# Key sums of stick-breaking attention in four products per head, a low-rank gate weight in one stationary block, and two gate rows spread by way of DRAM

## The chip, the cores and the metric

The kernel runs on one core of one Trainium2 chip. The metric is the device time of one execution in microseconds (us), as the median of several runs. Five engines work side by side, each in its own program order: TensorE (PE, the matrix products; its weight loads are listed as PEld), VectorE (DVE), ScalarE (ACT), GpSimd (POOL) and SyncE (SP, which here only starts transfers, one after the other).

## The reference, cut to what matters

One layer: adaLN modulation from a vector `c`, two token mixers side by side (gated linear attention, "GLA", and stick-breaking attention), an output projection, then a squared-ReLU MLP. 256 tokens, width 2048, all in float32.

```python
mod = silu(c) @ w_ada + b_ada;  sh1, sc1, g1, sh2, sc2, g2 = split(mod, 6)
h = rmsnorm(x, ng[0]) * (1 + sc1) + sh1
proj = h @ w_in               # q_a k_a v_a r_a a_low q_b k_b v_b gate_a gate_b
# GLA: log_a = log_sigmoid(a_low @ w_gate_up + b_gate) / 16   (a_low has 16 columns)
# stick-breaking, 16 heads of 128, query blocks of 128:
z = q @ k.T * 128 ** -0.5
log_1mb = where(past, log_sigmoid(-z), 0)
after = cumsum(log_1mb, reverse over keys) - log_1mb
w = where(past, exp(log_sigmoid(z) + after), 0);  o = w @ v
mixed = sigmoid(gate_a) * y_a + sigmoid(gate_b) * y_b
x = x + g1 * rmsnorm(mixed @ w_out, ng[1])
f = square(relu((rmsnorm(x, ng[2]) * (1 + sc2) + sh2) @ w_ff1)) @ w_ff2
x = x + g2 * rmsnorm(f, ng[3])
```

## The kernel before

Every float32 operand of a large product is split into a high part `h_...` (ACT, line 156) and a low part `l_...` (DVE, line 157). `mm_b_split` (line 166) does 16 steps over the inner dimension with two products each: the high weight block against 512 columns (256 tokens high, then 256 low) and the low weight block against the 256 high columns. `natural_block` (line 208) does three products of 512 columns per step. The weights come in loads of 1 MB started by SP (`load`, line 140) into the pool `wraw` with four buffers; their split halves go to the pool `wsp` with five buffers of each kind. A load waits on SP until the DVE has finished with the buffer that it takes. The modulation vector is worked out by DVE in 96 steps (`ada_step`, line 300, tiles `ad`) that are strewn between the products. A scheduler arranges each engine's order when the program is built; on the chip each engine keeps to it.

In order of time: the products of v and r (tile `pv`); the low-rank gate (lines 447 to 496); q and k of GLA per head (`pb_qa`, `pb_ka`); the GLA gates and outputs; q and k of stick-breaking (`pb_qb`, `pb_kb`) with the stages `sb_scores`, `sb_weights`, `sb_values` of earlier heads between them; the second gate and output (`pa_gb`, `pa_yb`); `w_out` (`pa_wo`); the MLP in eight parts (`pb_f`, `pa_f`).

Three places are touched.

**Key sums** (`sb_weights`, line 639). For each head, suffix sums over keys are products with a triangular matrix `uinc_r` and a matrix of ones, each for the high and the low part of `nl`. PSUM tile `pc` holds 384 columns: keys 0 to 127 against all 256 queries in columns 0 to 255, keys 128 to 255 against queries 128 to 255 in columns 256 to 383.

**Low-rank gate** (lines 448 to 480). The weight `a_low` of 16 columns is laid into zeroed blocks of 128 columns, high part `wl_h` and low part `wl_l`, and multiplied with `mm_b_split` (tile `pb_al`). The sum `alT` (16 rows and a row of ones for the bias) is the stationary operand of four products with `gup_sb` (tiles `gt`); ACT and DVE make `ls` from them, and `eg` are products with `ls`.

**Rows of g1 and g2** (`spread2`, line 280). A vector stands down the partitions (`G1c`, `G2c`, 128 x 16) and is wanted as a row of 2048 on every partition (`G1`, `G2`). DVE makes diagonal matrices `dg` (in a buffer of `wraw`), PE multiplies ones by them (`sp`), ACT copies out. Rows of g1 are first used by `mixed_out` (line 765), rows of g2 by `ff_out` in the last of the eight parts (line 820).

Of the kernel before, what the change touches and what calls it, by code (L numbers as in the profile page):

```python
# [8 lines left out]
F32 = mybir.dt.float32  # L9
F32R = mybir.dt.float32r  # L10
AF = mybir.ActivationFunctionType
ALU = mybir.AluOpType
PSUM = bass.MemoryType.PSUM

P = 128
D = 2048
T = 256
KT = D // P
# [19 lines left out]
def trunk_kernel(ctx, tc, xT, xn, cT, ada, bcol, ngcol, w_alow, w_gup, gg_row,  # L38
# [3 lines left out]
    v_, s_, g_, pe, dma = nc.vector, nc.scalar, nc.gpsimd, nc.tensor, nc.sync  # L42

    const = ctx.enter_context(tc.tile_pool(name="const", bufs=1))
    wraw = ctx.enter_context(tc.tile_pool(name="wraw", bufs=4))
    wsp = ctx.enter_context(tc.tile_pool(name="wsp", bufs=5))
# [10 lines left out]
    def pm(name):  # L57
        return ps_m.tile([P, 512], F32, tag="pm", name=name)

    def pw(name):  # L60
        return ps_w.tile([P, 512], F32, tag="pw", name=name)
# [215 lines left out]
                s_.copy(dst(n), ps[:, m])  # L277
        return made

    def spread2(cols, dst, name):  # L280

        dgs = wraw.tile([P, KT, P], F32R, tag="raw", name=f"dg_{name}")
        hi = const.tile([P, KT], F32R, name=f"ch_{name}")
        lo = const.tile([P, KT], F32, name=f"cl_{name}")
        v_.tensor_copy(hi, cols)
        v_.tensor_tensor(out=lo, in0=cols, in1=hi.bitcast(F32), op=ALU.subtract)
        for n in range(4):
            ps = pm(f"sp_{name}_{n}")
            for u, c in enumerate((hi.bitcast(F32), lo)):
                dg = dgs[:, 8 * (n % 2) + 4 * u:8 * (n % 2) + 4 * u + 4]  # L290
                v_.tensor_tensor(out=dg, in0=ident.unsqueeze(1).broadcast_to([P, 4, P]),
                                 in1=c[:, 4 * n:4 * n + 4].unsqueeze(2).broadcast_to([P, 4, P]), op=ALU.mult)
                pe.matmul(ps, ones_r, dg.rearrange("p k t -> p (k t)"), start=u == 0, stop=u == 1)
            s_.copy(dst(n), ps)

    cb = const.tile([P, D], F32, name="cb")
    with tc.high_priority():
# [147 lines left out]
    gp = ctx.enter_context(ExitStack())  # L445
    gl = gp.enter_context(tc.tile_pool(name="gl", bufs=1))
    if True:
        gup_sb = wraw.tile([P, 2048], F32, tag="raw", name="gup_sb")[0:17, 0:1024]
        s_.dma_start(gup_sb, w_gup)
        wl_r = gl.tile([P, KT, 16], F32, name="wl_r")  # L450
        s_.dma_start(wl_r, w_alow)
        parts = []
        for u in range(2):
            wl_h = wsp.tile([P, 8, P], F32R, tag="hi", name=f"wl_h{u}")
            wl_l = wsp.tile([P, 8, P], F32R, tag="lo", name=f"wl_l{u}")
            g_.memset(wl_h.bitcast(F32), 0.0)
            g_.memset(wl_l.bitcast(F32), 0.0)
            r = wl_r[:, 8 * u:8 * u + 8]
            s_.copy(wl_h[:, :, 0:16], r)
            v_.tensor_tensor(out=wl_l[:, :, 0:16], in0=r, in1=wl_h[:, :, 0:16].bitcast(F32), op=ALU.subtract)  # L460
            parts.append([t.rearrange("p k c -> p (k c)") for t in (wl_h, wl_l)])
        pl = mm_b_split(parts, hT, "al")

        al2 = evp.tile([P, T], F32, tag="e0", name="al2")[0:16]
        s_.copy(al2, pl[0:16, T:2 * T])
        alT = evp.tile([P, T], F32, tag="e1", name="alT", bufs=1)[0:17]
        v_.memset(alT, 1.0)
        v_.tensor_tensor(out=alT[0:16], in0=pl[0:16, 0:T], in1=al2, op=ALU.add)

        ls = [slot([1024], f"ls{i}") for i in range(NTOK)]  # L470
        for i in range(NTOK):
# [140 lines left out]
    with tc.tile_pool(name="sb", bufs=3) as sb:  # L612
        def sb_project(h):
            qk = []
            for w, nm in ((w_qb, "q"), (w_kb, "k")):
                t = sb.tile([P, T], F32, tag=f"s{nm}", name=f"s{nm}_{h}", bufs=2)
                ps = mm_b(w[h], hT, f"{nm}b_{h}")
                merge(t, ps, f"{nm}b_{h}", float(P) ** -0.5 if nm == "q" else None)
                ada_tick()
                qk.append(t)  # L620
            return qk

        def sb_scores(h, q, k):
            pz = pm(f"pz_{h}")
            pe.matmul(pz[:, 0:T], k[:, 0:P], q, start=True, stop=True)
            pe.matmul(pz[:, T:384], k[:, P:T], q[:, P:T], start=True, stop=True)
            z = sb.tile([P, 384], F32, tag="z", name=f"z_{h}", bufs=2)
            v_.tensor_tensor(out=z, in0=pz[:, 0:384], in1=negm, op=ALU.add)
            e = sb.tile([P, 384], F32, tag="e", name=f"e_{h}")
            s_.activation(e, z, AF.Abs)  # L630
            s_.activation(e, e, AF.Exp, scale=-1.0)
            s_.activation(e, e, AF.Ln, bias=onec)
            v_.scalar_tensor_tensor(out=e, in0=z, scalar=0.0, in1=e, op0=ALU.max, op1=ALU.add)
            nl = sb.tile([P, 2, 384], F32R, tag="nl", name=f"nl_{h}", bufs=2)
            s_.copy(nl[:, 0], e)
            v_.tensor_tensor(out=nl[:, 1], in0=e, in1=nl[:, 0].bitcast(F32), op=ALU.subtract)
            return z, e, nl

        def sb_weights(h, z, e, nl):
            pc = pm(f"pc_{h}")  # L640
            for u in range(2):
                pe.matmul(pc[:, 0:T], uinc_r, nl[:, u, 0:T], start=u == 0, stop=False)
            for u in range(2):
                pe.matmul(pc[:, P:T], ones_r, nl[:, u, T:384], start=False, stop=u == 1)
            for u in range(2):
                pe.matmul(pc[:, T:384], uinc_r, nl[:, u, T:384], start=u == 0, stop=u == 1)
            v_.scalar_tensor_tensor(out=z, in0=pc[:, 0:384], scalar=-1.0, in1=z, op0=ALU.mult, op1=ALU.add)
            s_.activation(e, z, AF.Exp)
            return e

        def sb_values(h, e):
            vv, j = vB[h // 4], h % 4
            po = pm(f"pob_{h}")
            pe.matmul(po[:, 0:T], vv[:, 0, j * P:(j + 1) * P], e[:, 0:T], start=True, stop=False)
            pe.matmul(po[:, P:T], vv[:, 1, j * P:(j + 1) * P], e[:, T:384], start=False, stop=True)
            split(oB, h, po[:, 0:T])

        stages = (sb_scores, sb_weights, sb_values)
        held = {}
        for t in range(SBH + 3):  # L660
            if t < SBH:
                held[t] = sb_project(t)
            for n, stage in enumerate(stages, 1):
                h = t - n
                if 0 <= h < SBH:
                    r = stage(h, *held[h])
                    held[h] = r if isinstance(r, tuple) else (r,)
# [42 lines left out]
    def G1(n):  # L710
        return G1t[n // 2][:, n % 2 * 512:(n % 2 + 1) * 512]

    spread2(G1c, G1, "G1")
    ss1 = endp.tile([P, NTOK, 4], F32, name="ss1")
    def rstd(ss, name):

# [65 lines left out]
    for b in range(FB):  # L782
# [23 lines left out]
        if b == FB - 1:  # L806
            while 5 not in done:
                next(jobs)
            G2t = [slot([1024], f"G2{u}") for u in range(2)]
            spread2(G2c, lambda n: G2t[n // 2][:, n % 2 * 512:(n % 2 + 1) * 512], "G2")  # L810
        for n in range(4):
            def ff_out(i, ps):
                f = fs(i, n)
# [83 lines left out]
```

## Time and profile before

| | us |
|---|---|
| median of 3 runs (1822.67 to 1823.84) | 1823.79 |
| the profiled execution, its own time | 1821.68 |
| span of the profiled execution, first to last instruction | 1820.0 |
| TensorE busy | 1780.8 (98%) |
| DVE busy | 1288.3 (71%) |
| ACT busy | 896.8 (49%) |
| POOL busy | 15.8 (1%) |
| moved by DMA | 428.51 MB, mean 235 GB/s |

The busy time of an engine is the time covered by its instructions. Matmuls are pipelined, so the time from the start of one to the start of the next tells what one costs; their own durations overlap. The chain that ended last runs 90% through PE, 5% through DVE and 2% through ACT.

### The profile page before, as it was taken

The numbers are of one execution on the slowest core, as the hardware profiler recorded it, in microseconds if no ns is written. First come the engines' busy times: TensorE is split into PE (matmuls) and PEld (weight loads), VectorE is DVE, ScalarE is ACT, GpSimd is POOL, SyncE is SP. The second block draws the span as 40 slices with busy tenths as digits, with TensorE's granted clock in tenths as the row PEclk, the third lists the DMA queues.
The fourth block names the chain that finished last, engine by engine and source line by source line (L and its number), as shares of the span: only waits on it lengthen the run. The fifth ranks groups of instructions, "written<-read, shape, count | busy, mean of one in ns | idle before, by whom it ended". The sixth has DMA issues, their size and how long they took to land.

```text
span 1820.0 us, 22246 instructions
## 1 busy us (share of the span) xinstructions
PE 1780.8 (98%) x8762; PEld 1485.5 (82%) x8762; DVE 1288.3 (71%) x1516; ACT 896.8 (49%) x1223; POOL 15.8 (1%) x34
## 2 busy tenths in 40 slices
PE   6999999999999999999999999999999999999997
PEld 4787787877888888888888878888888888888886
DVE  8898875887676677776677567676767666656565
ACT  6544544655653465555644455444444343444443
POOL 0000000000000000000000000000000000000000
PEclk8999999999999999999999999999999999999999
DMA  8898964565777766556776643565656666555542
GB/s 334 319 353 324 343 232 184 215 225 221 267 276 272 276 231 232 213 227 254 281 264 229 225 179 139 212 241 218 254 209 236 223 235 231 208 196 187 195 174 81
DMA packets 61179, 428.51 MB, mean 235 GB/s; under 512 B 7169, under 2 KB 7297, under 8 KB 9874
## 3 DMA queue, kind: packets, MB, share of 16 engines
q1 hardware_dynamic: 58896, 422.61, 62.7%
q10 hardware_dynamic: 2178, 4.48, 0.7%
q8 instruction: 69, 1.13, 0.2%
q14 instruction: 36, 0.29, 0.1%
HBM read 424.96 MB, written 2.10 MB: 235 GB/s over the span
## 4 chain that ended last, share of the span: by engine, by line
PE 90%; DVE 5%; issue 2%; ACT 2%; DMA 1%; POOL 0%; SPq 0%; POOLq 0%; DVEq 0%; ACTq 0%
PE pb_f L174 19%; PE pa_f L212 6%; PE pa_f L211 6%; PE pa_f L213 6%; PE pb_kb L174 5%; PE pb_qb L174 5%; PE pv L212 4%; PE pv L213 4%; PE pv L211 3%; PE pb_qa L174 2%; PE pb_ka L174 2%; PE pa_yb L213 2%; PE pa_yb L212 2%; PE pa_yb L211 2%; PE pa_ya L213 2%
## 5 line engine op out<-in xcount | busy, mean ns | idle before, releaser
L157 DVE TENSOR_TENSOR l_f<-r_f,h_f 128x1024 fp32r<-128x1024 f32 x256 | 312.7, 1224 | 181.3 <-ACT h_f L156 178.0
L156 ACT CAST h_f<-r_f 128x1024 fp32r<-128x1024 f32 x256 | 269.2, 1054 | 263.7 <-PE pa_f L213 193.7
L174 PE MATMUL pb_f<-h,h_f 128*128 128x512 f32 x992 | 346.8, 399 | 0.0
L174 PE MATMUL pb_f<-h,l_f 128*128 128x256 f32 x992 | 268.5, 281 | 0.0
L303 DVE SCALAR_TENSOR_TENSOR ad<-ad,cb 128x2048 f32<-128x2048 f32 x96 | 219.1, 2285 | 19.9 <-DMA ad<-in_ada_dram 19.7
L174 PEld LDWEIGHTS pb_f<-h,h_f 128*128 128x128 f32 x992 | 182.7, 188 | 40.4
L211 PE MATMUL pa_f<-h_f,ft 128*128 128x512 f32 x512 | 199.3, 389 | 0.0
L213 PE MATMUL pa_f<-h_f,ft 128*128 128x512 f32 x512 | 199.2, 389 | 0.0
L212 PE MATMUL pa_f<-l_f,ft 128*128 128x512 f32 x512 | 199.2, 389 | 0.0
L174 PEld LDWEIGHTS pb_f<-h,l_f 128*128 128x128 f32 x992 | 187.3, 189 | 6.1
L211 PE MATMUL pv<-h_v,hT 128*128 128x512 f32 x384 | 150.2, 396 | 9.8 <-ACT hT L370 7.1
L212 PE MATMUL pv<-l_v,hT 128*128 128x512 f32 x384 | 151.3, 396 | 3.4 <-DVE l_v L157 3.4
L213 PE MATMUL pv<-h_v,hT 128*128 128x512 f32 x384 | 150.1, 394 | 0.0
L156 ACT CAST h_v<-r_v 128x1024 fp32r<-128x1024 f32 x96 | 98.4, 1047 | 85.1 <-PE pv L213 46.1
L157 DVE TENSOR_TENSOR l_v<-r_v,h_v 128x1024 fp32r<-128x1024 f32 x96 | 115.1, 1219 | 32.6 <-ACT h_v L156 32.4
L213 PEld LDWEIGHTS pa_f<-h_f,ft 128*128 128x128 f32 x512 | 96.1, 188 | 19.9
L212 PEld LDWEIGHTS pa_f<-l_f,ft 128*128 128x128 f32 x512 | 96.1, 188 | 19.9
L211 PEld LDWEIGHTS pa_f<-h_f,ft 128*128 128x128 f32 x512 | 96.1, 188 | 19.8
L211 PEld LDWEIGHTS pv<-h_v,hT 128*128 128x128 f32 x384 | 73.0, 191 | 27.3 <-ACT hT L370 7.5
L174 PE MATMUL pb_qb<-hT,h_qb 128*128 128x512 f32 x256 | 91.7, 399 | 0.0
L174 PE MATMUL pb_kb<-hT,h_kb 128*128 128x512 f32 x256 | 90.6, 393 | 0.0
L212 PEld LDWEIGHTS pv<-l_v,hT 128*128 128x128 f32 x384 | 72.8, 190 | 21.5 <-DVE l_v L157 6.5
(272 smaller groups left out, 3306.2 us busy)
## 6 DMA issues: line engine op xcount, KB each, us to landing
r_f<-in_w_f_dram SPq DMA_DIRECT2D x128, 1024.0 KB, 4.8
ad<-in_ada_dram SPq DMA_DIRECT2D x96, 1024.0 KB, 5.2
r_v<-in_w_nat_dram SPq DMA_DIRECT2D x48, 1024.0 KB, 6.5
r_ga<-in_w_ga_dram SPq DMA_DIRECT2D x16, 1024.0 KB, 5.0
r_ya<-in_w_ao_dram SPq DMA_DIRECT2D x16, 1024.0 KB, 4.8
r_qb<-in_w_qb_dram SPq DMA_DIRECT2D x16, 1024.0 KB, 5.0
r_kb<-in_w_kb_dram SPq DMA_DIRECT2D x16, 1024.0 KB, 5.3
r_gb<-in_w_gb_dram SPq DMA_DIRECT2D x16, 1024.0 KB, 5.1
```

What stands on the lines that cost most here:

```text
L156: s_.copy(hi[:, 0:m], raw[:, o:o + m])
L157: v_.tensor_tensor(out=lo[:, 0:m], in0=raw[:, o:o + m], in1=hi[:, 0:m].bitcast(F32), op=ALU.subtract)
L174: pe.matmul(o, l, r, start=kt == 0 and n == 0, stop=kt == KT - 1 and n == 1)
L211: pe.matmul(ps, ah, w[0], start=start, stop=False)
L212: pe.matmul(ps, ah, w[1], start=False, stop=False)
L213: pe.matmul(ps, al, w[0], start=False, stop=stop)
L303: v_.scalar_tensor_tensor(out=raw, in0=raw, scalar=1.0, in1=cb, op0=ALU.mult, op1=ALU.mult, accum_out=mods[:, m, kt:kt + 1])
```

## The change

`sb_weights` multiplies all 384 columns by the triangular matrix at once, for the high and the low part, and then adds the ones products: four products per head in place of six. The low-rank weight has its high part in columns 0 to 15 and its low part in columns 32 to 47 of one stationary block, so that 16 products of 512 columns do the work of 32; the two results are on partitions 0 to 15 and 32 to 47 and stay apart: `alT` and `gup_sb` now have 48 rows, with the 16 rows of `w_gate_up` twice and zeros between, and the next product adds them. `rows` replaces `spread2`: one transpose to 16 partitions, one copy, one write of 8 KB to DRAM and two transfers that read 4 KB each onto all 128 partitions; all three stand in SP's queue.

```diff
-    def spread2(cols, dst, name):
-
-        dgs = wraw.tile([P, KT, P], F32R, tag="raw", name=f"dg_{name}")
-        hi = const.tile([P, KT], F32R, name=f"ch_{name}")
-        lo = const.tile([P, KT], F32, name=f"cl_{name}")
-        v_.tensor_copy(hi, cols)
-        v_.tensor_tensor(out=lo, in0=cols, in1=hi.bitcast(F32), op=ALU.subtract)
-        for n in range(4):
-            ps = pm(f"sp_{name}_{n}")
-            for u, c in enumerate((hi.bitcast(F32), lo)):
-                dg = dgs[:, 8 * (n % 2) + 4 * u:8 * (n % 2) + 4 * u + 4]
-                v_.tensor_tensor(out=dg, in0=ident.unsqueeze(1).broadcast_to([P, 4, P]),
-                                 in1=c[:, 4 * n:4 * n + 4].unsqueeze(2).broadcast_to([P, 4, P]), op=ALU.mult)
-                pe.matmul(ps, ones_r, dg.rearrange("p k t -> p (k t)"), start=u == 0, stop=u == 1)
-            s_.copy(dst(n), ps)
+    rowp = ctx.enter_context(tc.tile_pool(name="rowp", bufs=1, space=bass.MemoryType.DRAM))
+
+    def rows(cols, dst, name):
+
+        pt = pm(f"rt_{name}")
+        pe.transpose(pt[0:KT, 0:P], cols, ident)
+        t = evp.tile([P, T], F32, tag="half", name=f"rw_{name}")[0:KT, 0:P]
+        s_.copy(t, pt[0:KT, 0:P])
+        d = rowp.tile([KT, P], F32, name=f"rd_{name}")
+        dma.dma_start(d, t)
+        for u in range(2):
+            dma.dma_start(dst[u], d[8 * u:8 * u + 8].rearrange("k p -> (k p)").partition_broadcast(P))
...
-        gup_sb = wraw.tile([P, 2048], F32, tag="raw", name="gup_sb")[0:17, 0:1024]
-        s_.dma_start(gup_sb, w_gup)
+        gup_sb = wraw.tile([P, 2048], F32, tag="raw", name="gup_sb")[0:48, 0:1024]
+        g_.memset(gup_sb, 0.0)
+        s_.dma_start(gup_sb[0:17], w_gup)
+        s_.dma_start(gup_sb[32:48], w_gup[0:16])
         wl_r = gl.tile([P, KT, 16], F32, name="wl_r")
         s_.dma_start(wl_r, w_alow)
-        parts = []
+        pl = pw("pb_al")
         for u in range(2):
-            wl_h = wsp.tile([P, 8, P], F32R, tag="hi", name=f"wl_h{u}")
-            wl_l = wsp.tile([P, 8, P], F32R, tag="lo", name=f"wl_l{u}")
-            g_.memset(wl_h.bitcast(F32), 0.0)
-            g_.memset(wl_l.bitcast(F32), 0.0)
+            wl = wsp.tile([P, 8, P], F32R, tag="hi", name=f"wl{u}")
+            g_.memset(wl.bitcast(F32), 0.0)
             r = wl_r[:, 8 * u:8 * u + 8]
-            s_.copy(wl_h[:, :, 0:16], r)
-            v_.tensor_tensor(out=wl_l[:, :, 0:16], in0=r, in1=wl_h[:, :, 0:16].bitcast(F32), op=ALU.subtract)
-            parts.append([t.rearrange("p k c -> p (k c)") for t in (wl_h, wl_l)])
-        pl = mm_b_split(parts, hT, "al")
+            s_.copy(wl[:, :, 0:16], r)
+            v_.tensor_tensor(out=wl[:, :, 32:48], in0=r, in1=wl[:, :, 0:16].bitcast(F32), op=ALU.subtract)
+            for k in range(8):
+                kt = 8 * u + k
+                pe.matmul(pl, wl[:, k], hT[kt].rearrange("p a t -> p (a t)"), start=kt == 0, stop=kt == KT - 1)
...
-        v_.tensor_tensor(out=alT[0:16], in0=pl[0:16, 0:T], in1=al2, op=ALU.add)
+        for o in (0, 32):
+            v_.tensor_tensor(out=alT[o:o + 16], in0=pl[o:o + 16, 0:T], in1=al2[o:o + 16], op=ALU.add)
...
             for u in range(2):
-                pe.matmul(pc[:, 0:T], uinc_r, nl[:, u, 0:T], start=u == 0, stop=False)
+                pe.matmul(pc[:, 0:384], uinc_r, nl[:, u], start=u == 0, stop=False)
             for u in range(2):
                 pe.matmul(pc[:, P:T], ones_r, nl[:, u, T:384], start=False, stop=u == 1)
-            for u in range(2):
-                pe.matmul(pc[:, T:384], uinc_r, nl[:, u, T:384], start=u == 0, stop=u == 1)
...
-    spread2(G1c, G1, "G1")
+    rows(G1c, G1t, "G1")
...
-            spread2(G2c, lambda n: G2t[n // 2][:, n % 2 * 512:(n % 2 + 1) * 512], "G2")
+            rows(G2c, G2t, "G2")
```

On PE, in the stick-breaking stage, the products of one head's key sums stand between the scores of the next head (`pz`) and the next projection (`pb_qb`). Before:

```order
L626 MATMUL pz_4835<-sq_4628,sk_4675 128x128
L642 MATMUL pc_4848<-nl_4735,uinc_r 128x256 x2
L644 MATMUL pc_4848<-nl_4735,ones_r 128x128 x2
L646 MATMUL pc_4848<-nl_4735,uinc_r 128x128 x2
L174 MATMUL pb_qb_4868<-hT_207,h_qb_0_4860 128x512
```

and of the change:

```order
L626 MATMUL pz_4820<-sq_4613,sk_4660 128x128
L642 MATMUL pc_4833<-nl_4720,uinc_r 128x384 x2
L644 MATMUL pc_4833<-nl_4720,ones_r 128x128 x2
L174 MATMUL pb_qb_4851<-hT_209,h_qb_0_4843 128x512
```

Two products of 128 columns are gone, and the first two have 128 columns more; nothing else moved there.

On DVE, at the low-rank gate, the sum `alT` stands among the splits of the q and k weights (`l_qa`, `l_ka`), one modulation step (`ad`) and the first `ls`. Before:

```order
L157 TENSOR_TENSOR l_qa_1_0_2308<-r_qa_1_2305,h_qa_1_0_2307 128x1024
L303 SCALAR_TENSOR_TENSOR ad_0_2398,mods<-ad_0_2398,cb 128x2048
L157 TENSOR_TENSOR l_qa_1_1_2312<-r_qa_1_2305,h_qa_1_1_2311 128x1024
L468 TENSOR_TENSOR alT<-pb_al,al_2171 16x256
L157 TENSOR_TENSOR l_ka_0_0_2355<-r_ka_0_2352,h_ka_0_0_2354 128x1024
L480 SCALAR_TENSOR_TENSOR ls_2176<-gt_0_2178,g_0_0_2180 128x512
```

and of the change:

```order
L157 TENSOR_TENSOR l_qa_1_0_2293<-r_qa_1_2290,h_qa_1_0_2292 128x1024
L157 TENSOR_TENSOR l_qa_1_1_2297<-r_qa_1_2290,h_qa_1_1_2296 128x1024
L468 TENSOR_TENSOR alT<-pb_al,al_2155 16x256 x2
L300 SCALAR_TENSOR_TENSOR ad_0_2383,mods<-ad_0_2383,cb 128x2048
L157 TENSOR_TENSOR l_ka_0_0_2340<-r_ka_0_2337,h_ka_0_0_2339 128x1024
L480 SCALAR_TENSOR_TENSOR ls_2161<-gt_0_2163,g_0_0_2165 128x512
```

The sum is two instructions, and the modulation step has gone from ahead of it to behind it, ahead of the first `ls`.

On SP, at the start of `w_out`, the three transfers of `rows` stand among the loads of the weight (of the change; before, the loads follow each other without them):

```order
L142 DMA r_wo_0_7925<-in_w_out_dram 128x2048
L289 DMA rd_G_7759<-rw_G_7757 16x128
L142 DMA r_wo_1_7959<-in_w_out_dram 128x2048
L291 DMA G_7753<-rd_G_7759 128x1024
L291 DMA G_7754<-rd_G_7759 128x1024
L142 DMA r_wo_2_7993<-in_w_out_dram 128x2048
```

The write comes behind the fifth load of `w_out`, the two reads behind the sixth. For g2 the three stand together ahead of the last two loads of the kernel.

## Rows read from the trace of the kernel before

**Rows 1.** The page, part 1: busy us (share of the span) and instructions of each engine.
```profile
PE 1780.8 (98%) x8762; PEld 1485.5 (82%) x8762; DVE 1288.3 (71%) x1516; ACT 896.8 (49%) x1223; POOL 15.8 (1%) x34
```

**Rows 2.** Windows: length; PE, PEld, DVE, ACT, POOL busy (count); clock, DMA share, GB/s.
```profile
298.00:638.00 340.00, 339.09 (x1667) 274.78 (x1668) 243.46 (x291) 181.21 (x257) 5.13 (x7) 1.00 0.67 250
638.00:818.00 180.00, 179.52 (x1068) 158.81 (x1067) 136.38 (x181) 106.50 (x171) 0.00 (x0) 1.00 0.61 228
...
1010.00:1110.00 100.00, 95.07 (x487) 80.68 (x487) 63.06 (x97) 53.63 (x97) 2.76 (x4) 0.98 0.43 156
1110.00:1800.00 690.00, 690.00 (x3482) 584.87 (x3482) 455.59 (x549) 308.50 (x390) 0.00 (x0) 1.00 0.58 209
```

**Rows 3.** Timeline of PE in the low-rank product: start, duration, instruction.
```profile
298.82 0.39 PE L174 MATMUL pb_al<-hT,wl_h 128*128 128x512 f32 x1
299.05 0.28 PE L174 MATMUL pb_al<-hT,wl_l 128*128 128x256 f32 x1
299.17 0.39 PE L174 MATMUL pb_al<-hT,wl_h 128*128 128x512 f32 x1
```

**Rows 4.** Timeline of all engines behind the low-rank product.
```profile
301.55 2.29 DVE L303 SCALAR_TENSOR_TENSOR ad<-ad,cb 128x2048 f32<-128x2048 f32 x1 [2.17 <-DMA ad<-in_ada_dram]
...
304.23 0.36 ACT L465 COPY al<-pb_al 16x256 f32<-16x256 f32 x1 [1.84 <-PE pb_al L174]
...
304.91 0.40 DVE L468 TENSOR_TENSOR alT<-pb_al,al 16x256 f32<-16x256 f32 x1
...
305.76 2.84 PE L475 MATMUL gt<-gup_sb,alT 17*128 17x512 f32 x6
...
308.96 0.69 DVE L480 SCALAR_TENSOR_TENSOR ls<-gt,g 128x512 f32<-128x512 f32 x1 [2.17 <-ACT g L479]
```

**Rows 5.** Timeline, one head's key sums: weight loads (PEld) and products.
```profile
638.78 0.30 PEld L642 LDWEIGHTS pc<-nl,uinc_r 128*128 128x128 f32 x2
638.81 0.48 PE L642 MATMUL pc<-nl,uinc_r 128*128 128x256 f32 x2
...
639.02 0.31 PEld L644 LDWEIGHTS pc<-nl,ones_r 128*128 128x128 f32 x2
...
639.53 0.44 PE L174 MATMUL pb_qb<-hT,h_qb 128*128 128x512 f32 x1
```

**Rows 6.** Timeline of PE: a group of four transposes, then the spread of g1.
```profile
975.21 0.60 PE L678 MATMUL mt<-ident,m_ga 128*128 128x128 f32 x4
975.56 0.48 PE L211 MATMUL pa_yb<-h_yb,oB 128*128 128x512 f32 x1
975.88 0.39 PE L212 MATMUL pa_yb<-l_yb,oB 128*128 128x512 f32 x1
...
992.48 1.09 PE L293 MATMUL sp_G<-dg_G,ones_r 128*128 128x512 f32 x4
993.40 0.39 PE L211 MATMUL pa_wo<-h_wo,mx 128*128 128x512 f32 x1
```

**Rows 7.** SP from 960 to 1010 and 1776: its waits (total, times, longest) and issues.
```profile
SPq L142 <- PE sp_G L293: 10.8, 1, 10.8
...
986.85 0.33 SPq L142 DMA_DIRECT2D r_wo<-in_w_out_dram  x1
997.96 0.80 SPq L142 DMA_DIRECT2D r_wo<-in_w_out_dram  x2
...
1776.72 0.33 SPq L142 DMA_DIRECT2D r_f<-in_w_f_dram  x1
```

**Rows 8.** DMA issues by line: count, KB each, median us from issue to landing.
```profile
gg<-in_gg_row_dram ACTq DMA_DIRECT2D x4, 256.0 KB, 4.3
...
out_dram<-x SPq DMA_DIRECT2D x4, 256.0 KB, 2.6
```

**Rows 9.** Timeline, last MLP part: the spread of g2 on PE, its first use on DVE.
```profile
1763.93 1.08 PE L293 MATMUL sp_G<-dg_G,ones_r 128*128 128x512 f32 x4
...
1779.33 1.29 DVE L820 TENSOR_TENSOR f<-f,G 128x512 f32<-128x512 f32 x2
```

More of the change, by code (lines that the diff above doesn't have):

```diff
@@ L447, in trunk_kernel @@
     if True:
-        gup_sb = wraw.tile([P, 2048], F32, tag="raw", name="gup_sb")[0:17, 0:1024]
-        s_.dma_start(gup_sb, w_gup)
+        gup_sb = wraw.tile([P, 2048], F32, tag="raw", name="gup_sb")[0:48, 0:1024]
+        g_.memset(gup_sb, 0.0)
+        s_.dma_start(gup_sb[0:17], w_gup)
+        s_.dma_start(gup_sb[32:48], w_gup[0:16])
         wl_r = gl.tile([P, KT, 16], F32, name="wl_r")
         s_.dma_start(wl_r, w_alow)
-        parts = []
+        pl = pw("pb_al")
         for u in range(2):
-            wl_h = wsp.tile([P, 8, P], F32R, tag="hi", name=f"wl_h{u}")
-            wl_l = wsp.tile([P, 8, P], F32R, tag="lo", name=f"wl_l{u}")
-            g_.memset(wl_h.bitcast(F32), 0.0)
-            g_.memset(wl_l.bitcast(F32), 0.0)
+            wl = wsp.tile([P, 8, P], F32R, tag="hi", name=f"wl{u}")
+            g_.memset(wl.bitcast(F32), 0.0)
             r = wl_r[:, 8 * u:8 * u + 8]
-            s_.copy(wl_h[:, :, 0:16], r)
-            v_.tensor_tensor(out=wl_l[:, :, 0:16], in0=r, in1=wl_h[:, :, 0:16].bitcast(F32), op=ALU.subtract)
-            parts.append([t.rearrange("p k c -> p (k c)") for t in (wl_h, wl_l)])
-        pl = mm_b_split(parts, hT, "al")
-        al2 = evp.tile([P, T], F32, tag="e0", name="al2")[0:16]
-        s_.copy(al2, pl[0:16, T:2 * T])
-        alT = evp.tile([P, T], F32, tag="e1", name="alT", bufs=1)[0:17]
+            s_.copy(wl[:, :, 0:16], r)
[3 more added lines that the diff above has]
+                pe.matmul(pl, wl[:, k], hT[kt].rearrange("p a t -> p (a t)"), start=kt == 0, stop=kt == KT - 1)
+        al2 = evp.tile([P, T], F32, tag="e0", name="al2")[0:48]
+        s_.copy(al2, pl[0:48, T:2 * T])
+        alT = evp.tile([P, T], F32, tag="e1", name="alT", bufs=1)[0:48]
         v_.memset(alT, 1.0)
-        v_.tensor_tensor(out=alT[0:16], in0=pl[0:16, 0:T], in1=al2, op=ALU.add)
+        for o in (0, 32):
+            v_.tensor_tensor(out=alT[o:o + 16], in0=pl[o:o + 16, 0:T], in1=al2[o:o + 16], op=ALU.add)
         ls = [slot([1024], f"ls{i}") for i in range(NTOK)]
```

## The prediction

> **What bounds the kernel now.** I read the page's busy shares first: PE is busy 98% of the span, its weight loads 82%, DVE 71% [rows 1]. A busy PE can still hide waits, so next I read the windows by stretch [rows 2]. In the three stretches where the change works, PE has almost no hole: 339.09 of 340 us from the low-rank gate to the end of the first output, 179.52 of 180 in stick-breaking, 690.00 of 690 in the MLP. The granted clock is 1.00 there, the 2.4 GHz level, and the DMA engines are busy 0.58 to 0.67 of the time, so a PE that runs a little faster is not starved by them. Only the turn from `w_out` to the MLP has a hole (95.07 of 100), and no edit stands in it. So the reader is to see this: time taken off PE's stream at these places should come off the end, nearly one for one, unless the change puts a wait in its place. The rest of the working is then done in PE steps, from start to start of neighbouring products.
>
> A product of 512 columns steps by 0.23 us: four take 992.48 to 993.40, 0.92, in the spread of g1 [rows 6], and one 298.82 to 299.05 at the gate [rows 3]. That is 0.45 ns a column.
>
> **Low-rank gate.** Before, a pair of a high product (512 columns) and a low one (256) takes 298.82 to 299.17, 0.35 us [rows 3]. After, one product of 512 columns does for the pair, 0.23. That is 0.12 off, 16 times: **1.9 us**. Bounds: the low product's own step is also 0.12 (299.05 to 299.17), so I see no more than 2.0 and no less than 1.7 here.
>
> The stage behind it may give some back. The chain is: copy of `al` on ACT at 304.23 (0.36), sum `alT` on DVE at 304.91 (0.40), then the products `gt` on PE at 305.76 [rows 4]. Now the sum is two instructions, 0.40 more, while PE arrives one product (0.23) sooner, because eight and not nine projection products stand between. Against that, the sum before came late because DVE was held by the modulation step of 2.29 us at 301.55, which now stands behind the sum. Then it is late for somebody else: the split of a k weight and the first `ls` wait behind it, ACT's next gate functions share one buffer and wait for `ls`, and the products `eg` on PE wait for them. Two of the bounds are clear: nothing at best, and at worst the whole modulation step and the second sum on PE, 2.29 + 0.40 = 2.7 us. The split itself costs nothing: its weight is for a projection two blocks later, more than 10 us of PE work away. I take **0.5 us given back**, near the lower end, because the first `ls` started only at 308.96, 3.2 us behind the start of `gt` [rows 4], with ACT's three gate functions between, and that covers most of the step. The two zero fills fewer on POOL, the fill and the second transfer for `gup_sb` cost nothing: POOL is busy 1% [rows 1] and ACT, which issues these transfers, is idle for nearly half of that stretch [rows 2].
>
> **Key sums.** The number of columns does not change: 256+256+128+128+128+128 = 1024 before, 384+384+128+128 = 1024 after. If a product cost only its columns, the group would take 1024 x 0.45 ns = 0.46 us and nothing would be won. But the group takes from 638.81 to 639.53, 0.72 us [rows 5]. Each product has its own weight load, and two of these start 0.24 us after the two before them (638.78, 639.02), 0.12 each; six are 0.72, the whole group. So here the load sets the pace of a product that has fewer than about 270 columns. After, the two of 384 columns take 0.17 each (columns), the two of 128 take 0.12 each (load): 0.58. That is 0.14 off, 16 heads: **2.2 us**. Bounds: 0 if the columns decide, and 2 loads x 0.12 x 16 = 3.8 if the wider ones ride under the loads. I take the middle one, since it is what both rows give together: a step is the longer of the two.
> [...]
> Nothing waits sooner or later for this: key sums are read a head later by DVE, behind a whole projection.
>
> **Rows of g1 and g2.** Each spread takes eight products of 512 columns off PE: 4 in 0.92, so 1.84 us [rows 6]. In their place comes one transpose. Four transposes and a product of 512 columns take 975.21 to 975.88, 0.67, so a transpose is (0.67 - 0.23)/4 = 0.11 [rows 6]; this one has fewer columns to load, and I keep 0.11 (bounds 0.05, the columns alone, and 0.25, if it runs alone). Net 1.73 a spread, **3.5 us** for both (bounds 3.2 to 3.6). DVE loses twenty instructions and ACT six, which nobody waited for.
>
> The price could be in SP's queue. For g1: SP's write stands behind the fifth load of `w_out` and waits for ACT's copy, which comes behind PE's transpose where the spread stood, so at about 994 on the clock of before (992.48, the transpose, and a cast and the copy on ACT). Two loads and all that follow queue behind it. But before, SP stood still there too: the fifth load waited from 986.85 to 997.96, 10.8 us of it for PE to release the diagonal matrices' buffer [rows 7]. That buffer is free now, so the fifth load goes ahead of the write, and the sixth can follow at 994, earlier than the 998 of before. The reads then wait for the write to land: a store of 256 KB lands in 2.6 us [rows 8], and I take no more than that for 8 KB. A row read onto 128 partitions, 256 KB, lands in 4.3 us [rows 8]; each of the two here is 512 KB, so at most 8.6, and one behind the other 17.2. So the rows of g1 are there between 994 + 2.6 + 4.3 = 1001 and 1014, and they are wanted when the first quarter of `w_out` is done, 96 products of 0.23 behind 992, so at 1014. For g2 the spread stood at 1763.93 [rows 9], so the write goes out at about 1765, the reads land between 1772 and 1785, and the first multiplication with them stood at 1779.33 [rows 9]. If they land late, DVE stands still up to 6 us and the splits behind it too, while PE has up to two and a half blocks in hand (five split halves of `wsp`; a block is 24 products of 0.23, 5.5 us), some 13 us. The last two loads of the kernel queue behind these reads; the last went out at 1776.72 [rows 7] and is wanted only by the last quarter, over 20 us later. I put the detour at **0**; without that cover it would cost at most the 6 us.
>
> **Sum.** 1.9 - 0.5 + 2.2 + 3.5 = 7.1 us. The profiled execution took 1821.68 us, which gives 1814.6. It lies 2.1 us below the median of the runs, 1823.79, so for a median of runs I say **1816.7 us**, 0.4% less.
>
> **Rivals.**
> - *The columns decide in the key sums.* For it: the column count is the same, and PE at 98% busy looks full. Against it: the group takes 0.72 us where 0.46 would do. The sum is 4.9, the time 1818.9.
> - *The loads alone decide*, and the wide products ride under them: sum 8.7, time 1815.1. Against it: 512 columns step by 0.23, not 0.12.
> - *The gate stage gives the gain back*: the modulation step ahead of the first `ls` reaches PE through ACT's single buffer. For it: `gt` and `eg` stand at fixed places in PE's order, and the places were close before. Price up to 2.7 in place of 0.5: sum 4.9; 1818.9. With the columns deciding too, 2.7: 1821.1, no measurable change.
> - *The detour by DRAM makes it slower.* SP serves one queue; a read that waits for a landing stops all weight loads. It begins to cost when the rows of g2 hold DVE, or the last two loads SP, beyond PE's cover of some 13 us; it makes the kernel slower when the reads land 13 + 7.1 + 3.6 = 24 us behind 1779, at 1803. The rows of before give 1785 at worst, so the transfers would have to take twice the slowest reading above. Time then: 1827.4 and more.
>
> **How the numbers follow.** A measurement here tells about 0.2%, 3.6 us, from no change. Chances: forecast 0.64, columns 0.11, loads 0.07, gate stage 0.13, detour 0.05. Faster by more than 0.2% means below 1820.1: the forecast, the loads, nearly all of the columns case and some 0.05 of the gate case, 0.86 together. The rest of the gate and columns cases is no change, 0.09; slower is the detour, 0.05. The range goes from 1813.8 (key sums by loads alone, nothing given back, and a run in the lower part of the spread of runs shown) to 1820.0 (columns decide, and 1.6 given back at the gate).
>
> **What would show it.** In the trace of after: the low-rank product in 16 steps of 0.23; a key-sum group of 0.58 from its first product to the next projection's; one transpose in place of eight products at the starts of `w_out` and of the last MLP part; PE still filled in those stretches. A hole of PE before `gt` or `eg`, a group of 0.72, or DVE standing before the first use of g1 or g2 would each show a term wrong. The forecast fails as a whole if PE's stream shortens by 7 us and the span doesn't.

## The result, and the profile after

The changed kernel takes 1813.63 us (median of 4 runs, 1813.1 to 1816.3), against 1823.23 for the kernel before in the same series (4 runs): a ratio of 0.995, 95% interval 0.9937 to 0.9962. (The ratios here are worked out from all runs and can differ a little from the quotient of two medians.) It is faster, and by somewhat more than the 0.4% forecast. A second series gave 1815.04 against 1822.97 (first experiment below).

The profiled execution of the change is the slowest of its four runs: its span is 1814.5 us, its own time 1816.3. Set beside the profiled execution of before (1819.95 against 1814.54) that is only 5.4 us of span, and the stages tell why. In this table, a stage goes from the first (or last) start of one tile's products to that of the next, as the trace gives them; the last three columns are experiments described below.

| stage | before | after | after, again | key sums alone | gate alone | rows alone |
|---|---|---|---|---|---|---|
| first `pb_al` stands at | 298.40 | 301.50 | 299.95 | 300.73 | 300.84 | 300.57 |
| `pb_al` to `pa_ga` (gate, GLA heads) | 123.78 | 121.97 | 121.78 | 123.89 | 121.84 | 123.88 |
| `pa_ga` to `pb_qb` | 181.59 | 181.60 | 181.69 | 181.63 | 181.69 | 181.59 |
| `pb_qb` to `pa_gb` (14 of 16 key sums) | 206.77 | 205.27 | 205.27 | 205.27 | 206.77 | 206.77 |
| `pa_gb` to `pa_yb` (the last two) | 92.04 | 90.97 | 90.99 | 90.99 | 92.01 | 92.03 |
| `pa_yb` to `tr` (row of g1) | 182.61 | 180.90 | 180.89 | 182.61 | 182.61 | 180.90 |
| `tr` to the last `pb_f` | 678.50 | 678.14 | 678.57 | 678.11 | 678.56 | 679.23 |
| last `pb_f` to last `pa_f` (row of g2) | 45.58 | 43.66 | 43.66 | 45.56 | 45.56 | 43.67 |
| first `pb_al` to the end of the span | 1521.55 | 1513.05 | 1513.37 | 1518.74 | 1519.79 | 1518.67 |

Each stage with an edit in it got shorter, and no other did by more than its scatter: 1.81 + 1.50 + 1.07 + 1.71 + 1.92 = 8.0 us. The stage of the turn to the MLP varies by up to 1.1 us between executions without any edit in it. Ahead of `pb_al`, where nothing was edited, the profiled execution of after lost 3.1 us; there a stage ended between 298.4 and 301.5 in the executions seen, and before's profiled one was the earliest of all. So the spans understate the change, and the medians are the better measure.

The page of after, part 1, beside [rows 1]:

```profile
PE 1773.2 (98%) x8700; PEld 1477.4 (81%) x8700; DVE 1279.8 (71%) x1497; ACT 894.8 (49%) x1217; POOL 15.3 (1%) x33
```

PE has 62 products fewer and is busy 7.6 us less, at the same share. The windows of after, beside [rows 2] (same columns; the first two are shifted with the start):

```profile
301.00:641.00 340.00, 338.90 (x1662) 274.61 (x1663) 245.15 (x294) 183.28 (x259) 5.14 (x7) 1.00 0.67 250
640.00:820.00 180.00, 179.90 (x1045) 158.64 (x1044) 137.05 (x183) 106.43 (x174) 0.00 (x0) 1.00 0.61 230
1010.00:1110.00 100.00, 94.31 (x493) 79.85 (x492) 64.87 (x102) 55.35 (x99) 3.02 (x4) 1.00 0.45 167
1110.00:1800.00 690.00, 690.00 (x3479) 584.93 (x3478) 450.04 (x536) 305.47 (x384) 0.00 (x0) 1.00 0.58 209
```

PE stayed filled in these three stretches, and in the fourth with an edit too, from 818 to 1010 with the row of g1, where it is busy 192.00 of 192 us (before 191.75). In stick-breaking its hole even fell from 0.48 to 0.10 us.

Timeline of PE at the low-rank product of after, beside [rows 3]:

```profile
301.50 3.89 PE L461 MATMUL pb_al<-hT,wl 128*128 128x512 f32 x16 [1.41 <-DVE rA L404]
305.23 0.39 PE L174 MATMUL pb_qa<-hT,h_qa 128*128 128x512 f32 x1
```

Sixteen steps take 301.50 to 305.23, 3.73 us, or 0.233 each.

Timeline of all engines behind it, beside [rows 4]:

```profile
305.43 0.37 ACT L464 COPY al<-pb_al 48x256 f32<-48x256 f32 x1 [0.76 <-PE pb_al L461]
...
305.84 0.83 DVE L468 TENSOR_TENSOR alT<-pb_al,al 16x256 f32<-16x256 f32 x2
...
306.71 2.29 DVE L300 SCALAR_TENSOR_TENSOR ad<-ad,cb 128x2048 f32<-128x2048 f32 x1
...
309.19 0.73 ACT L479 ACTIVATE g<-g,onec 128x512 f32<-128x512 f32 x1
310.18 0.69 DVE L480 SCALAR_TENSOR_TENSOR ls<-gt,g 128x512 f32<-128x512 f32 x1
```

The modulation step now stands behind the sum, as the order had shown. With a split behind it (308.93, 1.22 us) it holds DVE until 310.15, and ACT's third gate function ends at 309.92: `ls` is late by about 0.25 us. No product on PE waited for that: from 295 to 640 PE has the same two waits as before, 1.4 us ahead of `pb_al` and 0.5 (before 0.4) ahead of `at`, later in the stage.

Timeline of PE and its weight loads in one head's key sums of after, beside [rows 5]:

```profile
640.08 0.30 PEld L642 LDWEIGHTS pc<-nl,uinc_r 128*128 128x128 f32 x2
640.11 0.60 PE L642 MATMUL pc<-nl,uinc_r 128*128 128x384 f32 x2
...
640.37 0.36 PEld L644 LDWEIGHTS pc<-nl,ones_r 128*128 128x128 f32 x2
...
640.54 0.33 PE L644 MATMUL pc<-nl,ones_r 128*128 128x128 f32 x2
640.65 0.19 PEld L174 LDWEIGHTS pb_qb<-hT,h_qb 128*128 128x128 f32 x1
640.71 0.45 PE L174 MATMUL pb_qb<-hT,h_qb 128*128 128x512 f32 x1
```

From first product to the next projection's: 0.60 us, against 0.72 before. From first load to the next projection's load: 640.08 to 640.65, 0.57. The same load before, which [rows 5] leave out:

```profile
639.47 0.19 PEld L174 LDWEIGHTS pb_qb<-hT,h_qb 128*128 128x128 f32 x1
```

That makes 638.78 to 639.47, 0.69, before.

Timeline of PE at the start of `w_out` after, beside [rows 6]: the transpose where the spread stood.

```profile
991.19 0.27 PE L285 MATMUL rt_G<-ident,G1c 128*16 128x128 f32 x1
991.22 0.47 PE L211 MATMUL pa_wo<-h_wo,mx 128*128 128x512 f32 x1
991.53 0.39 PE L212 MATMUL pa_wo<-l_wo,mx 128*128 128x512 f32 x1
```

The transpose and the product behind it step by 0.03 and 0.31; with a product's usual 0.23 that is 0.11 for the transpose.

SP's issues from 960 to 1010 after, beside [rows 7] (a row of several issues gives the time from the first to the last):

```profile
965.08 20.82 SPq L142 DMA_DIRECT2D r_wo<-in_w_out_dram  x5
992.62 0.34 SPq L289 DMA_DIRECT2D rd_G<-rw_G  x1
994.45 0.34 SPq L142 DMA_DIRECT2D r_wo<-in_w_out_dram  x1
994.90 1.09 SPq L291 DMA_DIRECT2D G<-rd_G  x2
```

DMA issues of the detour in the whole run after, beside [rows 8]: KB each, median us from issue to landing.

```profile
G<-rd_G SPq DMA_DIRECT2D x4, 512.0 KB, 5.0
...
rd_G<-rw_G SPq DMA_DIRECT2D x2, 8.0 KB, 2.6
```

Timeline of SP and DVE in the last MLP part after, beside [rows 9]:

```profile
1765.34 0.81 SPq L291 DMA_DIRECT2D G<-rd_G  x2
...
1774.06 1.29 DVE L818 TENSOR_TENSOR f<-f,G 128x512 f32<-128x512 f32 x2
```

The reads of g2 are issued at 1765.34 and 1765.7 and the longest of that pair landed in 5.0 us, so the row is there by 1770.7, some 3.4 us ahead of its first use. (This stage begins 3.35 us earlier on the clock of after: 1760.34 in place of 1763.69.)

### The profile page after: what moved, and what is told of

Its sections match the earlier page's. It is cut to its first block, busy times and chain, and to the rows that moved or that the text cites. A ratio compares the mean times of both kernels' runs of the same rounds, so it can differ in the third digit from the quotient of the medians.

```text
span 1814.5 us, 22110 instructions
## 1 busy us (share of the span) xinstructions
PE 1773.2 (98%) x8700; PEld 1477.4 (81%) x8700; DVE 1279.8 (71%) x1497; ACT 894.8 (49%) x1217; POOL 15.3 (1%) x33
## 4 chain that ended last, share of the span: by engine, by line
PE 88%; DVE 7%; issue 2%; ACT 2%; DMA 2%; POOL 0%; SPq 0%; POOLq 0%; DVEq 0%; ACTq 0%
PE pb_f L174 19%; PE pa_f L213 6%; PE pa_f L211 6%; PE pa_f L212 6%; PE pb_kb L174 5%; PE pb_qb L174 5%; PE pv L212 3%; PE pv L213 3%; PE pv L211 3%; PE pb_qa L174 2%; DVE ad L300 2%; DVE l_v L157 2%; PE pa_yb L211 2%; PE pa_yb L212 2%; PE pa_yb L213 2%
```

## The experiments

The experiments put three things to the test: the edits' time comes off PE's stream, narrow products go at the pace of their weight loads, and the detour by DRAM is hidden. The rivals are: columns alone set the pace; the gate stage gives its gain back; the rows' gain comes from SP's queue and not from PE; the detour is near to costing something.

**The change once more.** No edit, to see which of the differences stay.

> The change once more. The trace of the change began its low-rank product 3.1 us later than the trace of before (301.50 against 298.40), ahead of any edit. Theory: that is an accident of one execution, in the loads of the v products; then this profile shows a start of its own between 297 and 302, the stretch from the first low-rank product to the end again 1513 us, and a median of 9 us (8 to 10) below before. Rival: the change delays the start (the start is again at 301 to 302) and its median comes from elsewhere.

Measured: 1815.04 us (5 runs), ratio 0.9956 [0.9943, 0.9968]. Its first `pb_al` stands at 299.95 and from there to the end it takes 1513.37, 0.3 us more than in the first profile. So a start at 301.50 is not fixed by the change. The profiles alone don't settle it, since the two earliest of all (298.40, and 298.50 in the last experiment below) are of kernels without any of the three edits. But the medians speak against a delay: 1822.97 less the 1521.55 of before and 1815.04 less 1513.37 leave 301.4 and 301.7 us for what comes ahead of `pb_al` and outside the span.

**Key sums alone**, in the kernel before:

```diff
-                pe.matmul(pc[:, 0:T], uinc_r, nl[:, u, 0:T], start=u == 0, stop=False)
+                pe.matmul(pc[:, 0:384], uinc_r, nl[:, u], start=u == 0, stop=False)
...
-            for u in range(2):
-                pe.matmul(pc[:, T:384], uinc_r, nl[:, u, T:384], start=u == 0, stop=u == 1)
```

> Key sums in four products alone, all else as before. If the parts add, the stretch from the first pb_qb to the first pa_yb is 296.2 us in place of 298.8, 2.6 less, and the time 2.6 us below before. By the forecast's term it is 2.2. Rival, columns decide: 0. All other stages keep their length within 0.3 us.

Measured: 1821.28 us (11 runs, before 1822.97), ratio 0.9985 [0.9975, 0.9996]. In the trace, 14 heads give 1.50 us, 0.107 a head, and the stage of the last two heads gives 1.05. Two of 0.107 are 0.21 of that. Most of the rest are two waits of PE in that stage, which the kernel before has and this one has not; its list of PE's waits from 800 to 910 (in total, times, longest) reads:

```profile
PE pc L642 <- ACT nl L635: 0.5, 1, 0.5
PE pob L654 <- ACT e L648: 0.2, 1, 0.2
```

The same list is empty with the edit. PE's timeline at the place of the first, before:

```profile
811.55 0.39 PE L212 MATMUL pa_gb<-l_gb,hT 128*128 128x512 f32 x1
812.42 0.39 PE L642 MATMUL pc<-nl,uinc_r 128*128 128x256 f32 x1 [0.48 <-ACT nl L635]
```

and after:

```profile
812.03 0.39 PE L212 MATMUL pa_gb<-l_gb,hT 128*128 128x512 f32 x1
812.52 0.44 PE L642 MATMUL pc<-nl,uinc_r 128*128 128x384 f32 x1
```

Here the last heads have no q and k projection to hide behind. With the shorter key sums the program's order puts eight products of `pa_gb` ahead of this `pc` in place of five (the same in both traces with the edit), and the hole is gone. The prediction had no such term.

**Low-rank gate alone**, in the kernel before (the three edits of lines 448 to 468 as in the change):

```diff
-        pl = mm_b_split(parts, hT, "al")
+                pe.matmul(pl, wl[:, k], hT[kt].rearrange("p a t -> p (a t)"), start=kt == 0, stop=kt == KT - 1)
...
+        for o in (0, 32):
+            v_.tensor_tensor(out=alT[o:o + 16], in0=pl[o:o + 16, 0:T], in1=al2[o:o + 16], op=ALU.add)
```

> The low-rank weight in one stationary block alone. If the parts add, the stretch from the first low-rank product to the first pa_ga is 122.0 us in place of 123.8, 1.8 less; by the forecast 1.4. Rival, the gate stage gives it back: 0 to 0.5. Time 1.4 to 1.9 us below before.

Measured: 1821.46 us (11 runs), ratio 0.999 [0.9981, 0.9999]. The stage is 1.94 us shorter. The product itself went from 5.63 us (32 steps) to 3.73 (16 steps), 1.90; nothing is given back within the scatter of the stage (123.58 to 123.89 in the four profiles without this edit, 121.78 to 122.03 in the eight with it).

**Rows of g1 and g2 alone**, in the kernel before:

```diff
-    spread2(G1c, G1, "G1")
+    rows(G1c, G1t, "G1")
...
-            spread2(G2c, lambda n: G2t[n // 2][:, n % 2 * 512:(n % 2 + 1) * 512], "G2")
+            rows(G2c, G2t, "G2")
```

> The rows of g1 and g2 by way of DRAM alone. If the parts add, the stretch from the first pa_yb to the first tr is 1.7 us shorter (180.9) and from there to the end 2.4 shorter; by the forecast 1.7 each. Time 3.5 to 4.1 us below before. Rival, the detour's waits cost something that only the other edits hide: less than 3.0.

Measured: 1819.37 us (11 runs), ratio 0.9985 [0.9975, 0.9996]. The stage of g1 is 1.71 us shorter and that of g2 1.91, as in the full change. By stages the three parts alone give 2.55 + 1.94 + 3.62 = 8.1 us, and the change 8.0: they add. By the medians they give 1.7 + 1.5 + 3.6 = 6.8.

**Key sums in eight products** of 128 columns, in the changed kernel:

```diff
-            for u in range(2):
-                pe.matmul(pc[:, 0:384], uinc_r, nl[:, u], start=u == 0, stop=False)
+            for o in (0, T, P):
+                for u in range(2):
+                    pe.matmul(pc[:, o:o + P], uinc_r, nl[:, u, o:o + P], start=u == 0, stop=u == 1 and o != P)
```

> The changed kernel, but its key sums in eight products of 128 columns a head (each product of 384 columns cut in three): the same 1024 columns, twice the products. The output is the same. Load theory (a step is never shorter than 0.107 to 0.12 us, the pace that the six products before and the two of 128 columns after keep): a group takes 8 x 0.12 = 0.96 us in place of 0.62 to 0.71, so the stretch from the first query product of the later heads to pa_gb goes from 205.27 to about 210 us, and the whole kernel is 5 to 6 us longer than the changed one, about 1820. Column theory: 1024 columns as before, 205.3 to 205.5 us, and no difference in the time.

Measured: 1822.93 us (10 runs, before 1824.36), ratio 0.999 [0.9979, 1.0002]: nearly the whole gain is gone. From the first `pb_al` to the end it takes 1520.65 us, 7.6 more than the change. The stage of 14 heads takes 210.88 us, 5.6 more than the change. Its timeline of one head:

```profile
639.21 0.75 PEld L643 LDWEIGHTS pc<-nl,uinc_r 128*128 128x128 f32 x6
639.24 0.86 PE L643 MATMUL pc<-nl,uinc_r 128*128 128x128 f32 x6
...
639.88 0.30 PEld L645 LDWEIGHTS pc<-nl,ones_r 128*128 128x128 f32 x2
...
640.11 0.19 PEld L174 LDWEIGHTS pb_qb<-hT,h_qb 128*128 128x128 f32 x1
640.17 0.45 PE L174 MATMUL pb_qb<-hT,h_qb 128*128 128x512 f32 x1
```

Eight loads start within 639.21 to 640.11, 0.90 us, 0.113 each, for the same 1024 columns. This settles it against the column rival: the number of narrow products, each with its own load, sets their pace. That it is the load, and not another cost that each product has, is not shown, since here no product goes without a load. The 14 groups, from first product to the next projection's, take 12.96 us in place of 8.51 (0.93 and 0.61 each), 4.45 more. The other 1.2 of the 5.6 was not expected: the 16 products with `h_kb`, the high half of a head's k weights, take 3.78 us in place of 3.69 in 13 of the 16 heads (in the change 3.78 in the first two heads, 3.69 in all others). The last two heads add 2.0 us, 1.3 of it PE's waits for `nl`. The Trainium skill (TensorE: Matmul & The Clock Gate, LDWEIGHTS) gives 107 ns for such a load (128 columns/1.2), and these rows, 113 ns, are near it. The gap of N/2.4 + 2.5 ns that the Trainium skill gives on the same page (Back-to-back issue gap) is by its own words for a product by itself and leaves the load out; by that eight products would take 0.45 us, an estimate, and the rows have 0.90.

**Order wide, ones, wide, ones** of the four products, in the changed kernel:

```diff
             for u in range(2):
                 pe.matmul(pc[:, 0:384], uinc_r, nl[:, u], start=u == 0, stop=False)
-            for u in range(2):
                 pe.matmul(pc[:, P:T], ones_r, nl[:, u, T:384], start=False, stop=u == 1)
```

> The changed kernel, with its four key-sum products in the order wide, ones, wide, ones. The same products, the same output. If each step is by itself the longer of its load and its columns, the order is all one: 205.27 us, within 0.1, from the first query product of the later heads to pa_gb. If a load runs under the columns of the product ahead of it, so that a narrow product behind a wide one costs its columns alone, the group loses some 0.06 to 0.1 us: 14 heads give 203.9 to 204.4 us, and the time is 1 to 1.6 us less.

Measured: 1816.27 us (7 runs), ratio 0.9951 [0.9935, 0.9967]. Its weight loads in one head:

```profile
639.90 0.19 PEld L642 LDWEIGHTS pc<-nl,uinc_r 128*128 128x128 f32 x1
...
640.01 0.19 PEld L643 LDWEIGHTS pc<-nl,ones_r 128*128 128x128 f32 x1
...
640.19 0.19 PEld L642 LDWEIGHTS pc<-nl,uinc_r 128*128 128x128 f32 x1
...
640.30 0.19 PEld L643 LDWEIGHTS pc<-nl,ones_r 128*128 128x128 f32 x1
...
640.48 0.19 PEld L174 LDWEIGHTS pb_qb<-hT,h_qb 128*128 128x128 f32 x1
```

The loads step by 0.11, 0.18, 0.11 and 0.18: a narrow product takes its load, a wide one its columns, whatever the order, and the sum is 0.58 as with the change. So the narrow products get no cheaper behind the wide ones. The stage was yet 0.76 us longer (206.03), against both expectations; the products of the group are not it (9.96 us for all 16 heads, 9.93 with the change). In every second head from the fourth on, seven in all, the products with `h_kb` take 3.78 us in place of 3.69, 0.66 together, as they did in the run before in nearly every head. Why is open.

**Each row read four times**, in the changed kernel:

```diff
-        for u in range(2):
+        for u in list(range(2)) * 4:
             dma.dma_start(dst[u], d[8 * u:8 * u + 8].rearrange("k p -> (k p)").partition_broadcast(P))
```

> The changed kernel, with each of the two G rows read four times over from DRAM, so that the last rows land some 13 to 16 us later. The output is the same. Theory of the cover: the rows of g2 land at about 1785 to 1790 in place of 1774 or before, DVE stands 10 to 16 us ahead of its first multiplication with them, PE has some 13 us of split weights in hand, and so the stretch from the last split product to the last product of the MLP goes from 43.66 us to between 43.7 and 49; the first G costs nothing or under 1 us, because the first quarter of the output product covers it. Rival, no cover: each microsecond that DVE stands is one of PE, 53 to 60 us there. Rival, more cover than that: 43.7 and the same time as the changed kernel.

Measured: 1814.86 us (5 runs), ratio 0.9948 [0.9929, 0.9967]; 43.66 us in the stage of g2, the same as with the change. But it doesn't test the cover. The last reads were issued at 1780.5, and the first multiplication with g2 stands at 1783.4 and no longer at 1774.06: the scheduler had put four splits and two sums ahead of it, and DVE never stood for the rows. The next two runs hold DVE's order.

**The row of g2 read late, with DVE's order held**: two extra reads of its first half, and then five.

```diff
+            with ExitStack() as behind:
+                if name == f"f2_{FB - 1}_2_0" and u == 1:
+                    behind.enter_context(tc.issue_after(pin[-1].ins))
...
-        for u in range(2):
+        for u in [0, 1] + [0] * (times - 1):
```

> The changed kernel, with the first half of the g2 row read three times over from DRAM (two extra reads of 512 KB), and DVE's order held: the second half split of the third quarter's first weight may not go ahead of the first two multiplications with g2, which is where it stands in the changed kernel. The output is the same. The last extra read goes out behind the kernel's last weight load, at about 1772 on the clock of the changed kernel, and lands at about 1777, so DVE stands some 3 us ahead of the multiplication (1774 before). Theory of the cover: PE wants that half split at about 1785 (the third quarter's products start at 1782.4, and the half's 12 products of 0.23 us come first), and it is now made by about 1781: no cost, 43.7 us from the last split product to the last product of the MLP. Rival, no cover: 3 us there.

> As the run before it, but with five extra reads of the first half of the g2 row, and DVE's order held in the same way. Four of the five go out behind the last weight load, each waiting for the one before it if writes of one tile follow each other; the last then lands at 1784 to 1790. The multiplications with g2 (four of 0.7 us) and the held split (1.2 us) come behind it, so the split is made at 1788 to 1794, and PE wants it at about 1785. Theory of the cover (some 11 us from 1774, beyond which every microsecond is PE's): 3 to 9 us more from the last split product to the last product, 47 to 53 in place of 43.66. Rival, no cover: 10 to 16 us more. Rival, the reads never reach PE: 43.7.

With two extra reads: 1814.38 us (4 runs, before 1824.06), ratio 0.9944 [0.9925, 0.9963]. DVE's timeline shows it standing for the row:

```profile
1771.17 1.23 DVE L162 TENSOR_TENSOR l_f<-r_f,h_f 128x1024 fp32r<-128x1024 f32 x1 [0.29 <-ACT h_f L158]
1777.03 1.29 DVE L823 TENSOR_TENSOR f<-f,G 128x512 f32<-128x512 f32 x2 [4.64 <-DMA G<-rd_G]
```

4.64 us, and the stage took 43.66 us as ever: all covered. With five: 1825.16 us (10 runs), ratio 1.0006 [0.9996, 1.0015]; the stage took 53.41, 9.75 more, and the whole gain was lost. PE's waits in that stretch, then the timeline of PE and four windows (PE busy, count, granted clock, DMA share, GB/s):

```profile
PE pa_f L217 <- DVE l_f L162: 7.2, 1, 7.2
```

```profile
1792.87 0.80 PE L217 MATMUL pa_f<-l_f,ft 128*128 128x512 f32 x1 [7.25 <-DVE l_f L162]
1793.47 0.63 PE L218 MATMUL pa_f<-h_f,ft 128*128 128x512 f32 x1
```

```profile
1784.40:1785.40 1.00, 1.00 (x6) 1.00 0.42 156
1785.47:1792.80 7.33, 0.16 (x1) 0.86 0.21 72
1792.90:1797.60 4.70, 4.70 (x11) 0.50 0.02 3
1797.70:1802.70 5.00, 5.00 (x24) 1.00 0.00 0
```

DVE's timeline there, and below it the split that PE waited for as it stands in the change:

```profile
1789.18 2.50 DVE L823 TENSOR_TENSOR f<-f,G 128x512 f32<-128x512 f32 x4 [6.45 <-DMA G<-rd_G]
1791.60 5.76 DVE L162 TENSOR_TENSOR l_f<-r_f,h_f 128x1024 fp32r<-128x1024 f32 x5
```

```profile
1775.60 1.23 DVE L157 TENSOR_TENSOR l_f<-r_f,h_f 128x1024 fp32r<-128x1024 f32 x1 [0.25 <-ACT h_f L156]
```

The first multiplication stands at 1789.18. The change has it at 1774.06 with a start 0.69 us later, so it is 15.8 us late. The split behind it is 16.7 us late (1791.60 against 1775.60, and the same 0.69), because here four multiplications stand ahead of it and not two: the order was held only in part. In the change the split is done at 1776.83, and PE's first product with it stands at 1786.10, so the cover is about 9.3 us from the split's place. The two agree: 16.7 less 9.3 is 7.4, and by the starts of its products PE came 7.4 us late (the wait itself is 7.25). The other 2.3 of the 9.75 are the granted clock. After that wait PE came back at 0.50, the 1.2 GHz level, and made eleven products, most at 0.43 us a step in place of 0.23, before 1.00 returned. The Trainium skill (TensorE: Matmul & The Clock Gate, Back-to-back issue gap) has N/1.2 at that level, 427 ns for 512 columns, and the rows agree.

**Diagonal matrices in a buffer of their own**, in the kernel before:

```diff
-        dgs = wraw.tile([P, KT, P], F32R, tag="raw", name=f"dg_{name}")
+        dgs = dgp.tile([P, KT, P], F32R, tag="dg", name=f"dg_{name}")
```

> The kernel before, with the diagonal matrices of its spreads in a buffer of their own in place of the one that the weight loads take turns in. The output is the same. Theory: SP's wait of 10.8 us for the spread of g1 goes, the loads of the output weights are issued earlier, and no stage gets shorter: the time is that of the kernel before within 0.3%, 1821 to 1825, so none of what the change won came from SP's queue. Rival: the wait held the loads of the output weights long enough for PE to feel it; the stage from the v-transposed output to the turn gets shorter than 182.6 us by over 0.3.

Measured: 1823.93 us (10 runs, before 1824.36), ratio 1.0 [0.9985, 1.0016]. SP's wait of 10.8 us for `sp_G` [rows 7] is gone from the list, and its loads of `w_out` start at 966.36 in place of 970.69:

```profile
966.36 39.59 SPq L142 DMA_DIRECT2D r_wo<-in_w_out_dram  x8
```

But SP stood as long as before: in the list one wait of 10.9 us has come in its place, for DVE's splits of `w_out` (total, times, longest):

```profile
SPq L142 <- DVE l_wo L157: 28.5, 5, 10.9
```

The first five loads go out 4 to 11 us earlier (the fifth at 986.86 in place of 997.96), the sixth and all behind it when they did before (998.15 and 998.38). No stage got shorter by it beyond the scatter (from `pa_yb` to `tr` 182.69 us, 182.61 before). So none of the rows' gain came from the loads that the diagonal matrices held back.

## Why the prediction was right, point by point

**PE is the bound and has no cover to lose.** Right. Products taken from its stream came off the stages, nearly one for one, in every part alone and in the whole. The wait of 1.4 us that PE has ahead of `pb_al` stayed.

**Low-rank gate, 1.9 us.** Right: 1.90 by its product's steps. *The 0.5 given back* was wrong: nothing was, within the scatter (stages 1.75 to 2.00 us shorter over the runs with the edit). The step that failed is the last link of its chain, "the products `eg` on PE wait for them". `ls` was late by 0.25 us, and no product waited for it. The rival with 2.7 us back fell with it.

**Key sums, 2.2 us.** The mechanism held and both its rivals fell: a step is the longer of a fixed 0.11 us, put down to the load, and its columns (eight products: 0.90; order changed: 0.58). The size was off in both directions. The 0.72 of before was taken from the first product's start, while 0.58 was built up from load steps. By load starts, before takes 0.69 and after 0.57, so that a head wins 0.11 and not 0.14: 1.7 us for 16. On top came 0.85 that no term had: the last two heads, where before's PE stood 0.48 and 0.25 us. There the prediction's sentence "nothing waits sooner or later for this" holds only while a projection stands behind each head.

**Rows, 3.5 us.** 3.62 measured; the transpose costs the 0.11 taken for it, and the spread of g2 had cost 1.95 us, a little more than the 1.84 taken from that of g1. **The detour, 0**: right. The reads landed in 3.9 to 7.0 us, one of them faster than the least that the forecast had (4.3 to 8.6). The rows of g2 were there by 1770.7, which is 1774.1 on the clock of before, within the 1772 to 1785 given. What the prediction had wrong is the margin. It gave PE 13 us in hand from five split halves. Measured are some 9.3 us from the place of the first split behind the multiplications, with a lower clock to pay beyond that. The scheduler's order is a second guard: told of longer reads, it moved the multiplications back.

**The sum.** 7.1 us forecast, 8.0 measured by stages. The medians of the two series differ by 9.6 and 7.9 us. For the time itself, 1816.7 was said and 1813.63 measured, 0.2 below the 1813.8 at which the range began. As a gain over before in one series it lies inside, near the end: 9.6 us (7.9 in the second series), with 3.8 to 10.0 forecast (1823.79 less the two ends of the range). That end had been drawn for wide products that ride under their loads, which was not the case, so a time so near to it is in part luck. Of the 3.1 us between forecast and measurement, 0.9 is in the terms, and the rest is put down to the scatter of short series (the medians of the change and of two runs that left its stages alone lie between 1813.63 and 1815.04) and of before's median, which stood at 1823.79 when the sum was made and at 1823.23 beside the change.

## What to carry to other kernels

On a PE that is full, cost a group of narrow products that each have a weight load of their own by the larger of 0.11 us (as here) and the columns (0.45 ns each), from load start to load start; fewer and wider products then pay even at equal columns. Compare stages between tile starts, not spans: an unedited stage here moved by 3 us between executions, more than most of the edits were worth. And before calling a transfer hidden, look how far its use stands from the work that PE wants behind it, and test that with the order held, since a scheduler told of a longer transfer moves the use.

## What the runs showed of the hardware

- A wait of 7.25 us on PE costs more than itself: eleven products behind it ran at a granted clock of 0.50 and lost 2.3 us, a third again.
- Products can step slower with no wait in sight: the 16 with `h_kb` took 3.78 us in place of 3.69 in heads where the order or the number of the key-sum products was another. That was worth 0.7 us (seven heads) and 1.2 us (13 heads).
- The first 300 us differ between executions with the same order of PE's products: a group of four products of `sp_cb` took 1.98 us in the profiled execution of before and 3.78 in that of after, and the first `pv` stood at 21.61 and 22.67; then PE waited 2.6 us for `h_v` in the one and 5.5 in the other, while the DMA engines were busy 0.86 and 0.84 of the time from 21 to 100. What decides this was not tried.
